# A hybrid decoder layer on one core: the feed-forwards of three token groups taken in the order 768, 768, 576 instead of 576, 768, 768

## The chip, the cores and the metric

The kernel runs on one core of a Trainium2 chip. The metric is the device time of one execution in microseconds: the median of repeated runs. Beside it stands one execution taken with the hardware profiler, whose trace gives the start and duration of every instruction of PE (TensorE matmuls; PEld are its weight loads), DVE (VectorE), ACT (ScalarE), POOL (GpSimd) and of the DMA queue that SP (SyncE) issues.

## The reference, cut to what matters

One decoder layer, in float32, over 2048 tokens of a prompt and 8 x 8 tokens of a sample group with the same weights. The model width is 1024, the feed-forward 4096.

```
h  = rmsnorm(x, norm_mix_w)
m  = mixer(h, ...)                 # retention and gated recurrence along the tokens, then @ w_out
x  = x + m
h  = rmsnorm(x, norm_ffn_w)
x  = x + square(relu(h @ w_up)) @ w_down       # 1024 -> 4096 -> 1024
y  = rmsnorm(x, final_norm_w)
```

Mixing runs along the tokens, since each carries a recurrent state to the next. The feed-forward treats each token by itself.

## The kernel before, in words

**Groups.** The 2112 tokens are cut into three groups, `gs[0]` of 64 sample and 512 prompt tokens (576), `gs[1]` and `gs[2]` of 768 prompt tokens. The program mixes them in turn (`mix`, `out_proj`), then runs a feed-forward (`ffn`) for each in turn. `out_proj` leaves two DRAM tensors per group: `fin`, the scaled input of the feed-forward, and `fres`, the residual. Tokens lie along the free dimension; each group is halved, so a matmul streams 288 or 384 columns. The program holds a second, slower copy of itself behind a flag (`judge` computes it); that copy isn't executed here.

**Products.** A float32 operand is split into two parts, hi and lo, and a product is hi x hi + hi x lo + lo x hi: three matmuls. The multiplication by `w_up` and `w_down` follows a scheme of seven products for a 2 x 2 block matrix, with sums of operands (T1 to T4) and of weights (S1 to S4, made earlier and kept in DRAM). Here a product means the 24 matmuls with one weight tile of 128 x 1024. A feed-forward is 112 products: 56 in the up half (eight rounds `t` of seven; `up_two` does the first two together, `up` the others), 56 in the down half (`down`, four octets).

**What each weight costs.** A tile is loaded into `raw` (8 buffers) by SP, copied to `hi` by ACT (L311) and the rest put into `lo` by DVE (L318). `hi` and `lo` have three buffers each, so the hi of product k+2 can be written once product k-1 is done, and its lo must be there for the third matmul of product k+2. The cost does not depend on the group.

**What else a feed-forward does, beside the matmuls (L1868).**
- `prepare` and `plan_operands` load quarters of `fin` (L1941, tile `ld`), form T1 to T4 (L1972, DVE) and split them (L1961 on ACT, L1965 on DVE).
- The results of products are added out of PSUM by DVE: L2087 and L2117 in `up_two`, L2145 in `up`, L2217 ("put") and L2220 in `down`; L2060 squares on DVE.
- `scale_residual(g, wait)` loads the residual from `fres`, squares it (L2003 on ACT, L2005 on DVE), sums it over the partitions (L2038, then `parts` L682 on ACT and L683 on DVE, matmuls L688 and L689) and scales it (L2020). `wait` is 0 in the first feed-forward and 190 in the others.
- `finish(g, ...)` belongs to the group just done and runs beside the next group's up half: squares (L2307 on ACT, L2309 and L2312 on DVE), the same column sum (L2038, L682, L683), then the multiplication by the final norm's factor (L2325, sixteen of half a group's width) and the write of y (L2327).
- The last group has no feed-forward behind it. `finish(g, (1,), True)` does its second token half during the last products. `last_rows` (L2367 on ACT, L2369 and L2372 on DVE), `last_product` and `finish_last` (squares L2407, L2408, L2412 and some recorded as L246, weights L2401 and L2403, sums L2427, factor L2358 and L2359, output multiplies L2436, writes L2437) do the first half around the last two products.

**What sets the order.** Such side work is put on an agenda by `later(ticks, ...)`; a tick is two matmuls, so it passes faster in the group of 576. Each engine runs its instructions in a fixed order, which a scheduler sets when the program is built; instructions recorded by a helper that raises their priority (`soon`) all carry line L246. The end of mixing is `out_proj(gs[2], 3, ...)`: eight projections whose results DVE adds to blocks of x (L246; `slab<-x` is their load, L252), in two PSUM buffers named pj, then eight short ones; during the first eight `prepare` begins loading the first feed-forward's operands.

```
            self.ffn(gs[0], lambda: self.prepare(gs[1], 8))
            self.finish(gs[0], begin=96, pace=10, wait=200, each=8)
            self.ffn(gs[1], lambda: self.prepare(gs[2], 8), 190)
            self.finish(gs[1], begin=96, pace=10, wait=200, each=8)
            ...
            self.ffn(gs[2], None, 190)
```

Of the kernel before, what the change touches and what calls it, by code (L numbers as in the profile page):

```python
# [205 lines left out]
class Kernel:  # L206
# [298 lines left out]
    def build(self):  # L505
        nc, tc, I = self.nc, self.tc, self.I
        with ExitStack() as ctx:
# [45 lines left out]
            gs = []  # L553
            off = 0
            for ns, p0, n in GROUPS:
# [4 lines left out]
                first = nch // 2  # L560
# [47 lines left out]
                mixing.close()  # L608
                self.pf = ctx.enter_context(tc.tile_pool(name="pf", bufs=2, space=bass.MemoryType.PSUM))

            self.out_proj(gs[2], 3, lambda: self.prepare(gs[0], 12), end_of_mixing)
            if self.fast:
                self.last_states()
            nc.sync.dma_start(self.O["ret_p"].rearrange("h d v -> d h v"), self.S[:, :H])
            nc.sync.dma_start(self.O["hg_p"].rearrange("h d v -> d h v"), self.S[:, H:])
            self.ffn(gs[0], lambda: self.prepare(gs[1], 8))
            self.finish(gs[0], begin=96, pace=10, wait=200, each=8)
            self.ffn(gs[1], lambda: self.prepare(gs[2], 8), 190)
            self.finish(gs[1], begin=96, pace=10, wait=200, each=8)
            if self.fast:  # L620
                self.judge()
            self.ffn(gs[2], None, 190)
            if self.fast:
                self.again = nc.values_load(self.flag, min_val=0, max_val=1,
                                            skip_runtime_bounds_check_because="a comparison's result is 0 or 1")
# [1879 lines left out]
```

## Time and profile before

| | |
|---|---|
| median of 3 runs | 2357.23 us (2357.16 to 2358.59) |
| the profiled execution | 2359.45 us, span of its instructions 2357.6 us |
| TensorE clock granted | 0.998 of full speed |
| busy: PE, DVE, ACT | 2337.3 us (99%), 1792.8 us (76%), 1227.3 us (52%) |
| feed-forward of 576 tokens | 1050 to 1408 us from the span's start |
| feed-forwards of 768 tokens | 1408 to 1874 and 1874 to 2340 us |
| moved by DMA | 575.6 MB, 244 GB/s on average |

Times in the trace count from the span's start. A line `L318 DVE TENSOR_TENSOR lo<-raw,hi` is an instruction of line 318 of the kernel on DVE, which writes a tile named lo from raw and hi; in brackets behind it stands how long the engine was idle before it and what ended that. Durations of neighbouring DVE or PE instructions overlap a little, so the step from one to the next is shorter than the printed duration.

### The profile page before, as it was taken

What the parts mean: (1) busy time and instruction counts of PE and PEld (TensorE: products, weight loads), DVE (VectorE), ACT (ScalarE), POOL (GpSimd) and SP (SyncE); (2) the same over time, 40 slices, a digit from 0 to 9 for tenths busy, and PEclk for the clock granted to TensorE, in tenths of its full rate; (3) what the DMA queues carried; (4) which work ended last, traced back from release to release, by engine and by line L of the source; (5) the groups of instructions that cost most, each with busy time, mean ns of one, the idle gap of its engine ahead of it and who ended that gap; (6) DMA issues with size and microseconds to landing.
All of it is one profiled execution on the core that took longest, in us unless ns stands there. A gap on an engine that the chain in (4) does not pass through costs nothing.

```text
span 2357.6 us, 39360 instructions
## 1 busy us (share of the span) xinstructions
PE 2337.3 (99%) x15340; PEld 2301.6 (98%) x15340; DVE 1792.8 (76%) x2309; ACT 1227.3 (52%) x1976; POOL 139.1 (6%) x199
## 2 busy tenths in 40 slices
PE   9999999999999999999999999999999999999998
PEld 8888899999999999999999999999999999999997
DVE  8766766777666776668769988666988787669887
ACT  5556555557645555546455546444544364445443
POOL 3221201111001100100000000000000000000000
PEclk9999999999999999999999999999999999999999
DMA  9888887779866777898677665767665458675642
GB/s 317 285 296 298 267 314 255 280 266 324 302 226 242 273 285 286 300 344 304 219 258 262 219 219 189 248 206 229 224 194 186 152 192 270 194 232 179 207 154 70
DMA packets 232649, 575.60 MB, mean 244 GB/s; under 512 B 24195, under 2 KB 92803, under 8 KB 232454
## 3 DMA queue, kind: packets, MB, share of 16 engines
q1 hardware_dynamic: 231766, 572.20, 71.3%
q8 instruction: 122, 2.00, 0.4%
q10 hardware_dynamic: 688, 0.80, 0.1%
q14 instruction: 73, 0.60, 0.1%
HBM read 419.95 MB, written 151.66 MB: 242 GB/s over the span
## 4 chain that ended last, share of the span: by engine, by line
PE 93%; DVE 3%; ACT 1%; DMA 1%; issue 1%; POOL 0%; SPq 0%; DVEq 0%; POOLq 0%; ACTq 0%
PE pj L1868 36%; PE pf L1868 28%; PE pj L464 11%; PE pj L1125 10%; PE pj L1206 2%; PE mm L1707 1%; PE mm L1715 1%; PE mm L1709 1%; PE mm L1393 1%; PE mm L1482 1%; PE mm L1635 1%; PE mm L1206 0%; PE mm L1857 0%; DVE raw L429 0%; DVE lo L318 0%
## 5 line engine op out<-in xcount | busy, mean ns | idle before, releaser
L1868 PE MATMUL pj<-slab,hi 128*128 128x384 f32 (+1 forms) x3504 | 853.4, 326 | 0.0
L311 ACT CAST hi<-raw 128x1024 fp32r<-128x1024 f32 x446 | 468.6, 1051 | 692.1 <-PE pj L1868 264.6
L318 DVE TENSOR_TENSOR lo<-raw,hi 128x1024 fp32r<-128x1024 f32 x446 | 545.8, 1224 | 157.3 <-ACT hi L311 152.2
L1868 PE MATMUL pf<-slab,hi 128*128 128x384 f32 (+1 forms) x2768 | 652.2, 321 | 0.0
L1868 PEld LDWEIGHTS pj<-slab,hi 128*128 128x128 f32 x3504 | 614.3, 188 | 0.0
L1868 PE MATMUL pj<-slab,lo 128*128 128x384 f32 (+1 forms) x1752 | 570.7, 326 | 0.0
L1868 PEld LDWEIGHTS pf<-slab,hi 128*128 128x128 f32 x2768 | 480.0, 188 | 0.1
L1868 PE MATMUL pf<-slab,lo 128*128 128x384 f32 (+1 forms) x1384 | 443.1, 320 | 0.0
L1868 PEld LDWEIGHTS pj<-slab,lo 128*128 128x128 f32 x1752 | 329.3, 188 | 0.0
L1125 PE MATMUL pj<-hi,slab 128*128 128x256 f32 x1344 | 260.4, 287 | 0.3 <-DVE slab L246 0.3
L1868 PEld LDWEIGHTS pf<-slab,lo 128*128 128x128 f32 x1384 | 260.1, 188 | 0.0
L464 PE MATMUL pj<-slab,hi 128*128 128x288 f32 (+1 forms) x1216 | 243.4, 316 | 2.1 <-ACT slab L246 1.0
L1125 PEld LDWEIGHTS pj<-hi,slab 128*128 128x128 f32 x1344 | 214.9, 191 | 0.6 <-DVE slab L246 0.6
L464 PEld LDWEIGHTS pj<-slab,hi 128*128 128x128 f32 x1216 | 194.2, 188 | 5.3 <-issue 1.8
L1125 PE MATMUL pj<-lo,slab 128*128 128x256 f32 x672 | 190.1, 283 | 0.0
L1961 ACT CAST slab<-slab 128x768 fp32r<-128x768 f32 (+1 forms) x192 | 145.4, 779 | 62.9 <-DVE slab L1972 47.4
L246 DVE TENSOR_TENSOR slab<-pj,slab 128x768 f32<-128x768 f32 (+2 forms) x136 | 124.2, 915 | 70.4 <-PE pj L1868 27.3
L1965 DVE TENSOR_TENSOR slab<-slab 128x768 fp32r<-128x768 f32 (+1 forms) x192 | 167.3, 886 | 13.2 <-ACT slab L1961 4.6
L464 PE MATMUL pj<-slab,lo 128*128 128x288 f32 (+1 forms) x608 | 143.5, 315 | 0.0
L1125 PEld LDWEIGHTS pj<-lo,slab 128*128 128x128 f32 x672 | 128.7, 192 | 0.0
L464 PEld LDWEIGHTS pj<-slab,lo 128*128 128x128 f32 x608 | 102.6, 188 | 0.3 <-issue 0.2
L2217 DVE TENSOR_TENSOR slab<-pf,slab 128x768 f32<-128x768 f32 (+1 forms) x87 | 76.5, 884 | 24.4 <-PE pf L1868 24.2
(265 smaller groups left out, 2572.0 us busy)
## 6 DMA issues: line engine op xcount, KB each, us to landing
raw<-w SPq DMA_DIRECT2D x254, 512.0 KB, 5.2
slab<-fu SPq DMA_DIRECT2D x64, 384.0 KB, 5.3
fu<-ld SPq DMA_DIRECT2D x60, 384.0 KB, 3.9
ld<-fin SPq DMA_DIRECT2D x28, 384.0 KB, 5.0
ld<-x SPq DMA_DIRECT2D x24, 384.0 KB, 7.0
slab<-fu SPq DMA_DIRECT2D x32, 288.0 KB, 4.8
fu<-ld SPq DMA_DIRECT2D x30, 288.0 KB, 3.2
slab<-x SPq DMA_DIRECT2D x16, 384.0 KB, 6.7
```

The costliest lines, as they stand in the source:

```text
L246: return fn(*a, **k)
L311: self.nc.scalar.copy(self.wts[j][0], raw)
L318: self.nc.vector.tensor_tensor(out=lo, in0=raw, in1=hi.bitcast(F32), op=ALU.subtract)
L464: self.nc.tensor.matmul(pj[:, i, :T2], w, a[:, c0:c1], start=j == 0 and q == 0, stop=j == n - 1 and q == 2)
L1125: self.nc.tensor.matmul(ps[:, tb * 256:(tb + 1) * 256], t, w[:, cols], start=first and kb == j == 0 and tb != 1, stop=kb == KB // 2 - 1 an ...
L1206: nc.tensor.matmul(dst, t[:, s:s + C], ww, start=kb == 0 and q == 0, stop=last and q == 2, skip_group_check=True)
L1393: nc.tensor.transpose(ps[:, j * P:(j + 1) * P], src[:, c], self.ident)
L1482: nc.tensor.matmul(ps[:, j * P:(j + 1) * P], k[:, cols[c]], q[:, cols[c]], start=True, stop=True)
L1868: m = self.nc.tensor.matmul(*a, **k)
L1961: self.nc.scalar.copy(hi[:, :g.T], B[name][:, :g.T])
L1965: self.nc.vector.tensor_tensor(out=lo[:, :g.T], in0=B[name][:, :g.T], in1=hi.bitcast(F32)[:, :g.T], op=ALU.subtract)
L2217: nc.vector.tensor_tensor(out=r, in0=ps, in1=r, op=ALU.add)
```

## The change

The feed-forwards run for `gs[1]`, `gs[2]`, `gs[0]`; with them go the preparation of operands, the finish and the program's last work, which is now that of the group of 576. Mixing keeps its order. In the changed kernel every line from 612 on has a number one higher.

```
-            self.out_proj(gs[2], 3, lambda: self.prepare(gs[0], 12), end_of_mixing)
+            first, second, third = (gs[1], gs[2], gs[0]) if self.fast else gs
+            self.out_proj(gs[2], 3, lambda: self.prepare(first, 12), end_of_mixing)
...
-            self.ffn(gs[0], lambda: self.prepare(gs[1], 8))
-            self.finish(gs[0], begin=96, pace=10, wait=200, each=8)
-            self.ffn(gs[1], lambda: self.prepare(gs[2], 8), 190)
-            self.finish(gs[1], begin=96, pace=10, wait=200, each=8)
+            self.ffn(first, lambda: self.prepare(second, 8))
+            self.finish(first, begin=96, pace=10, wait=200, each=8)
+            self.ffn(second, lambda: self.prepare(third, 8), 190)
+            self.finish(second, begin=96, pace=10, wait=200, each=8)
...
-            self.ffn(gs[2], None, 190)
+            self.ffn(third, None, 190)
```

Three places in the engines' orders, each before and then after the change.

SP's queue at the end of mixing, from the third-last block of x (`slab<-x`) on; `ld<-fin` are operands of the first feed-forward, `raw` weights, `fsd30S` and `fsd31S` sums of weights that are kept. Before:

```order
L1941 DMA ld<-fin_3781 128x2x288
L252 DMA raw<-w 128x1024
L1898 DMA raw<-w 128x1024
L252 DMA slab<-x 128x768
L1906 DMA fsd30S_11505<-raw 128x1024
L1906 DMA fsd31S_11597<-raw 128x1024
L252 DMA raw<-w 128x1024
L252 DMA slab<-x 128x768
L252 DMA raw<-w 128x1024
L1941 DMA ld<-fin_3781 128x2x288 x4
L252 DMA raw<-fsu0S_4699 128x1024
L252 DMA slab<-x 128x768
```

SP's queue at the same place, after:

```order
L1942 DMA ld<-fin_7765 128x2x384
L252 DMA raw<-w 128x1024
L1899 DMA raw<-w 128x1024
L252 DMA slab<-x 128x768
L1907 DMA fsd30S_11505<-raw 128x1024
L1942 DMA ld<-fin_7765 128x2x384
L1907 DMA fsd31S_11597<-raw 128x1024
L252 DMA slab<-x 128x768
L252 DMA raw<-w 128x1024 x2
L1942 DMA ld<-fin_7765 128x2x384 x2
L252 DMA raw<-fsu0S_4699 128x1024
L252 DMA slab<-x 128x768
```

One operand load and one block of x stand earlier, and four wider operand loads stand where five stood.

DVE in `up_two` of the last feed-forward, where it does that group's additions and the finish of the group before (L2309, L2312; L2310, L2313 after). Before, both groups have 768 tokens:

```order
L318 TENSOR_TENSOR lo<-raw,hi 128x1024
L2312 TENSOR_TENSOR slab<-slab 128x384
L2117 TENSOR_TENSOR slab<-slab 128x768
L2087 TENSOR_TENSOR slab<-pj,slab 128x768
L318 TENSOR_TENSOR lo<-raw,hi 128x1024
L2309 TENSOR_TENSOR slab<-slab 128x768 x2
L683 TENSOR_TENSOR slab<-slab 128x384
L2087 TENSOR_TENSOR ld<-pf,slab 128x768
L2087 TENSOR_TENSOR slab<-pf,slab 128x768
L318 TENSOR_TENSOR lo<-raw,hi 128x1024
```

DVE at the same place, after:

```order
L318 TENSOR_TENSOR lo<-raw,hi 128x1024
L2088 TENSOR_TENSOR slab<-pj,slab 128x576
L2118 TENSOR_TENSOR slab<-slab 128x576
L318 TENSOR_TENSOR lo<-raw,hi 128x1024
L2310 TENSOR_TENSOR slab<-slab 128x768
L2088 TENSOR_TENSOR ld<-pf,slab 128x576
L2310 TENSOR_TENSOR slab<-slab 128x768
L2088 TENSOR_TENSOR slab<-pf,slab 128x576
L318 TENSOR_TENSOR lo<-raw,hi 128x1024
L2310 TENSOR_TENSOR slab<-slab 128x768
```

The group's own rows are narrower, the finish of the group before and the weights' lo are as wide as before.

DVE at the program's end, around the last put (L2217, L2218 after) ahead of `last_product`; L246 are additions of its four blocks. Before:

```order
L318 TENSOR_TENSOR lo<-raw,hi 128x1024
L2325 SCALAR_TENSOR_TENSOR slab<-slab,vec 128x384
L2372 TENSOR_TENSOR slab<-slab 128x384
L2325 SCALAR_TENSOR_TENSOR slab<-slab,vec 128x384 x2
L2217 TENSOR_TENSOR slab<-pf,slab 128x768
L2325 SCALAR_TENSOR_TENSOR slab<-slab,vec 128x384 x2
L2369 TENSOR_TENSOR slab<-slab 128x768
L246 TENSOR_TENSOR slab<-pj,slab 128x384
L2325 SCALAR_TENSOR_TENSOR slab<-slab,vec 128x384 x2
L246 TENSOR_TENSOR slab<-pj,slab 128x384
L2325 SCALAR_TENSOR_TENSOR slab<-slab,vec 128x384
L2408 TENSOR_TENSOR slab<-slab 128x768
```

DVE at the same place, after:

```order
L318 TENSOR_TENSOR lo<-raw,hi 128x1024
L684 TENSOR_TENSOR slab<-slab 128x288
L2218 TENSOR_TENSOR slab<-pf,slab 128x576
L2373 TENSOR_TENSOR slab<-slab 128x288
L2326 SCALAR_TENSOR_TENSOR slab<-slab,vec 128x288 x2
L246 TENSOR_TENSOR slab<-pj,slab 128x288
L2326 SCALAR_TENSOR_TENSOR slab<-slab,vec 128x288 x2
L246 TENSOR_TENSOR slab<-pj,slab 128x288
L2370 TENSOR_TENSOR slab<-slab 128x576
L2326 SCALAR_TENSOR_TENSOR slab<-slab,vec 128x288 x2
L246 TENSOR_TENSOR slab<-pf,slab 128x288
L2409 TENSOR_TENSOR slab<-slab 128x576
```

All eight output multiplies L2326 of the finish now stand behind the put (two more follow the last row shown); before, three of the eight L2325 stood ahead of it.

## The prediction

> **What bounds the kernel now.** I began with the page's engine totals, then the stages of the feed-forwards, then the chain that ended last.
>
> ```profile
> span 2357.6 us, 39360 instructions
> PE 2337.3 (99%) x15340; PEld 2301.6 (98%) x15340; DVE 1792.8 (76%) x2309; ACT 1227.3 (52%) x1976; POOL 139.1 (6%) x199
> ...
> 1050.00:1229.30 179.30, 179.30 (x1346) 179.20 (x1346) 133.44 (x154) 98.00 (x123) 0.00 (x0) 1.00 0.79 265
> 1229.30:1408.40 179.10, 179.10 (x1345) 179.10 (x1345) 171.69 (x210) 94.25 (x116) 0.00 (x0) 1.00 0.73 238
> 1408.40:1641.40 233.00, 233.00 (x1348) 233.00 (x1347) 162.90 (x180) 114.51 (x134) 0.00 (x0) 1.00 0.66 214
> 1641.40:1874.40 233.00, 233.00 (x1346) 233.00 (x1345) 204.63 (x215) 104.87 (x117) 0.00 (x0) 1.00 0.60 195
> 1874.40:2107.30 232.90, 232.90 (x1346) 232.90 (x1345) 164.59 (x179) 115.18 (x133) 0.00 (x0) 1.00 0.66 215
> ...
> 1242.76 6.40 PE pf L1868 x48
> ...
> 1651.68 8.32 PE pj L1868 x48
> ```
>
> The five stage rows (length, then busy us of PE, PEld, DVE, ACT, POOL, then clock, DMA share, GB/s) are the up and down halves of the 576-token feed-forward, the same of the first one of 768, and the up half of the last. PE is busy through all of them at full clock. The two chain rows give the price of work there: 48 matmuls of 288 columns take 6.40 us (133 ns each), 48 of 384 columns 8.32 us (173 ns). One product is 24 matmuls against one weight: 3.20 us for the small group, 4.16 us for a big one. So TensorE bounds every feed-forward in either order, and what the change can move is only (a) the passage from mixing into the first feed-forward, (b) whatever makes PE wait inside one, (c) the end, where PE has finished and others have not.
>
> The profiled execution took 2359.45 us, 1.85 us around its 2357.6 us span. The sum below is made against that span; the median of the three runs, 2357.23, lies 2.2 us under the profiled time, and I add the sum to it.
>
> **PE work: 0.** The same 2688 matmuls of 288 and 2 x 2688 of 384 columns run, in another order. 358.4 + 2 x 465.9 us stays.
>
> **(a) The passage out of mixing: +0.3 us.** The first feed-forward's operands are now 384 KB quarters, not 288 KB ones. They are loaded beside the end of mixing, on SP's queue among the x blocks that the last residual adds wait for.
>
> ```profile
> 980.00:1000.00 20.00, 20.00 (x140) 20.00 (x139) 9.72 (x26) 8.90 (x39) 0.60 (x3) 1.00 0.85 331
> 1000.00:1020.00 20.00, 20.00 (x122) 19.97 (x121) 16.29 (x24) 6.96 (x11) 0.00 (x0) 1.00 0.95 303
> 1020.00:1040.00 20.00, 20.00 (x116) 19.73 (x115) 11.92 (x13) 4.56 (x5) 0.00 (x0) 1.00 0.99 345
> ...
> 1034.28 0.96 DVE L246 TENSOR_TENSOR slab<-pj,slab 128x768 f32<-128x768 f32 x1 [2.40 <-DMA slab<-x]
> ...
> 1034.83 0.51 PE L464 MATMUL pj<-slab,lo 128*128 128x384 f32 x2
> 1035.29 0.98 PE L464 MATMUL pj<-slab,hi 128*128 128x384 f32 x4
> ```
>
> The DMA engines are 99% busy, and the last add before PE reuses that PSUM bank waits 2.40 us for its x block. PE starts its next block at 1035.29, 0.46 us after the row before it; two such matmuls need 0.34, so it already waits 0.12 us here. There is no slack: what delays this x block delays PE. In the new order (front section) four operand loads stand ahead of that block in this stretch where five stood: 4 x 393 KB against 5 x 295 KB, 98 KB more, 0.28 us at the 345 GB/s of the third row. I take +0.3. The six loads before them grow by 590 KB, 1.7 us at that rate; between 980 and 1000 the DMA engines were idle 15% of 20 us, 3 us, which takes that in. If it didn't, the upper end is +1.9. At the lower end the 0.12 us vanishes, since one x block and one load moved ahead: -0.1. Behind this, the weights of the first products come 4.16 instead of 3.20 us apart while each still takes the same DMA, ACT and DVE time, so the first feed-forward is looser than before.
>
> **(b) DVE in the last feed-forward: +0.9 us.** The 576-token group leaves DVE least room: each weight costs it the same, and a product lasts 3.20 us. Its up half was first and carried only its own work. Now it carries the previous group's finish, with rows of 768. The step from one DVE row to the next is 0.08 us less than the printed duration, since they overlap.
>
> ```profile
> 1060.77 1.23 DVE L318 TENSOR_TENSOR lo<-raw,hi 128x1024 fp32r<-128x1024 f32 x1 [0.64 <-ACT hi L311]
> ...
> 1099.28 1.22 DVE L318 TENSOR_TENSOR lo<-raw,hi 128x1024 fp32r<-128x1024 f32 x1
> ...
> 1049.99 0.42 PE L1868 MATMUL pf<-slab,hi 128*128 128x288 f32 x2
> ...
> L2309 DVE TENSOR_TENSOR slab<-slab 128x768 f32<-128x768 f32 x6 | 5.7, 954 | 1.0 <-ACT slab L2307 0.9
> ...
> L2309 DVE TENSOR_TENSOR slab<-slab 128x576 f32<-128x576 f32 x6 | 4.5, 754 | 0.9 <-ACT slab L2307 0.8
> ...
> L2312 DVE TENSOR_TENSOR slab<-slab 128x384 f32<-128x384 f32 x2 | 1.1, 550 | 0.0
> L2325 DVE SCALAR_TENSOR_TENSOR slab<-slab,vec 128x384 f32<-128x384 f32 x16 | 8.8, 612 | 0.0
> ```
>
> The two L318 rows are the second halves ("lo") of the weights of products 5 and 17 of the first feed-forward; PE's product 0 begins at 1049.99. Between them lie 38.5 us, of which DVE works 34.1 (12 lo at 1.14, 30 rows of 576 elements at 0.67, one of 288 at 0.37). In the new order the same stretch of the last feed-forward gets six L2309 (0.87 each), two L2312, two L2038 and two L683 of 384 elements (0.47 each), 8.0 us, and loses three L2005 and one L2038 (2.4): 39.7 us of DVE work where PE needs 12 x 3.20 = 38.4. The lo of product 17 may begin at latest 0.27 us into its product less its own 1.14: 54.4 - 0.9 = 53.5 us after the first product begins; that of product 5 begins at 10.8. Room 42.7, work 39.7, and the waits of DVE for ACT's hi (0.64 in the first row; about that before each of the next five weights, 3.2 in all) leave -0.2. A wait of L2309 for ACT, 0.9 in its row, makes it -1.1. I take a PE wait of 0.9 us, near the second, since in the order L2309 follows its square on ACT closely. Bounds: 0, when those waits vanish because DVE is behind the hi anyway; 2.3, when the whole 4.4 us of idle time between the two rows stays and the 0.9 comes on top (42.7 - 39.7 - 4.4 - 0.9). After product 17 the sixteen L2325 (0.53 each) come, but L2005 moves away: 22.9 us of work in the 25.6 us of the next eight products, so it recovers. The down half of the 576 group ran without a PE wait at 171.7 of 179.1 us and now loses the six rows of preparing a next group.
>
> **(c) The end: +0.2 us.**
>
> ```profile
> 2334.00 0.61 DVE L2325 SCALAR_TENSOR_TENSOR slab<-slab,vec 128x384 f32<-128x384 f32 x1
> ...
> 2336.28 0.96 DVE L2217 TENSOR_TENSOR slab<-pf,slab 128x768 f32<-128x768 f32 x1
> 2337.16 1.14 DVE L2325 SCALAR_TENSOR_TENSOR slab<-slab,vec 128x384 f32<-128x384 f32 x2
> ...
> 2344.09 0.56 DVE L246 TENSOR_TENSOR slab<-slab 128x384 f32<-128x384 f32 x1
> 2344.23 0.34 PE L1868 MATMUL pf<-slab,lo 128*128 128x384 f32 x1
> ...
> 2344.70 1.63 PE L2427 MATMUL pj<-slab,ones 128*128 128x192 f32 x8
> 2345.00 0.63 ACT L246 ACTIVATE slab<-slab 128x192 f32<-128x192 f32 x2 [0.29 <-DVE slab L246]
> 2346.80 3.84 DVE L2436 TENSOR_TENSOR slab<-slab 128x384 f32<-128x384 f32 x8 [0.72 <-ACT slab L2359]
> 2348.32 1.78 SPq L2437 DMA_DIRECT2D y<-slab  x2
> ...
> GB/s 0 0 0 0 0 0 0 0 0 222 340 0 200 356 7 50 380 134 360 200 0 0 0 0 23 0 0 192 356 358 371 368 357 216 68 26 18 12 0 0
> ```
>
> From the top: DVE takes the last put before `last_product` (2336.28) and then works nearly without a gap to the third sum at 2344.09. PE's last matmul begins at 2344.23. The column sums (L2427) need both and start at 2344.70; ACT's squares of the last block end at 2345.63 and the second half of the sums waits for them; the output multiplies start at 2346.80, the output DMAs at 2348.32. In the GB/s row (0.7 us a slice from 2330) they fill the DMA engines from 2348 to 2353.
>
> The PE total is unchanged, so PE's last matmul comes at the same time, but its last two products take 2 x 3.20 instead of 2 x 4.16: the DVE chain behind the last put starts 1.92 us later. It does not get shorter by as much. In the new order it holds three rows of 576 elements, six of 288, two of 144 and eight L2325 of 288; before, only five of the eight L2325 stood behind the put. By the two L2309 rows an element costs 1.04 ns and a row 0.15 us beside; so the steps are 0.67, 0.37, 0.22 and, for L2325 (0.612 less 0.10 for 96 elements), 0.43: 2.0 + 2.2 + 0.4 + 3.4 = 8.1, with 0.1 for the start 8.2 us, against 8.4 before (2336.28 to 2344.70). The sums start 1.92 - 0.2 = 1.7 us later. From there to the first output multiply it took 2.10; the wait of the second sums for ACT (0.9) goes, since the squares now lie before the third sum, but both Ln now stand ahead of both Exp, and I take 0.4 off. From the first output multiply to the end it took 10.8; 4 x 393 KB are written at about 360 GB/s in 4.4 us, 4 x 295 KB in 3.3: 1.1 off. Sum 1.7 - 0.4 - 1.1 = +0.2. Bounds: -1.7, if DVE keeps up with PE and the sums start where they did with 0.4 + 1.3 off behind them (1.3 with the first two multiplies, 0.2); +1.3, if DVE waits 0.6 more for ACT and the shorter multiplies (8 x 0.10) set the rest in place of the bytes.
>
> [...] Were the rows proportional to their elements instead, the chain of 8.4 us would be 8.4 x 0.75 plus the three moved L2325, 7.5 us, and the end 0.7 us sooner than I have it.
>
> [...]
>
> **Sum.** +0.3 +0.9 +0.2 = +1.4 us: span 2359.0, and 2357.23 + 1.4 = 2358.6.
>
> **Rivals.** Within 0.2% is 4.7 us either way, about what a measurement can tell here.
> - *The small tail pays.* Nothing new waits and the end shrinks with the group. For it: PE's own last two products are 1.92 shorter. Against it: PE's total isn't, and DVE's chain binds. All of the 13.0 us from PE's end (2344.6) to 2357.6, at three quarters, gives -3.3: 2353.9. Even so it is not faster by 0.2%; for that (under 2352.5) the end must lose 4.7 of its 13.0 us, for which I see no row. Chances 0.15 and 0.03.
> - *DVE and ACT trade waits in the last feed-forward (slower).* If each of the twelve lo between products 5 and 17 waits 0.64 us for its hi, as the first six do, 7.7 us of idle time stand against a room of 3.0: PE waits 4.7 us, and with 0.3 and 0.2 the time is 2362.4. It decides from 7.2 us of idle time there on. Against it: once DVE is behind, the hi are long done; from 1078 on before it hardly idles. Chance 0.11.
> - *The DMA backlog persists into the passage.* (a) becomes 1.9: 2360.2. For it: 95% and 99% DMA. Against it: the idle 15% before. Chance 0.10.
> - *The edit does nothing.* The orders show that it moves all it names; but with no wait anywhere and an even end the time is 2357.2, inside the likeliest case.
>
> **How the numbers follow.** The likeliest case, 0.61, has its own range of 2356.5 to 2360.5, from (b) between 0 and 2.3 and (c) about one us either way. The given range, 2354.0 to 2362.0, leaves out the lower half of the first rival (0.07 and 0.03) and most of the second (0.08). Only the 0.03 is faster by over 0.2%, only the second rival slower (over 2361.9): 0.03, 0.86, 0.11.
>
> **What would show it.** Right: the feed-forwards stand as two of 465.9 us and one of about 359, the PE gap near the last x block is 0.1 to 0.7 us, DVE is full in the first 70 us of the last feed-forward with a lo landing late near products 13 to 17, and from PE's last matmul to the column sums 2 us pass where 0.1 did. Wrong: PE gaps elsewhere (operands or weights not landed at a change of group), a gap of over 2 us in the last up half, or sums that start at once behind PE.

## The result, and the profile after

The changed kernel takes 2362.14 us (median of 22 runs, 2358.99 to 2364.78), the kernel before 2358.66 us in 22 runs beside it (2356.87 to 2360.42; the three shown ahead are among them). The ratio is 1.0015, with a 95% interval of 1.0009 to 1.0021: 3.5 us slower, where 1.4 were forecast. That is within the 0.2% that was called no change, and 0.1 us above the upper end of the range. The profiled execution took 2361.42 us, 0.7 below its median; its span is 1.9 us longer than before.

I read three places, in the order of the prediction's steps. Line numbers from 612 on are one higher in the changed kernel. First the passage. The DVE rows below are, for the kernel before and then for the changed one, an update of the state in mixing, ahead of the first moved instruction, and the last residual add, at which the first feed-forward begins.

```profile
905.22 0.29 DVE L246 SCALAR_TENSOR_TENSOR S<-S,mm 128x128 f32<-128x128 f32 x1 [0.24 <-PE mm L1715]
...
1050.19 0.96 DVE L246 TENSOR_TENSOR slab<-pj,slab 128x768 f32<-128x768 f32 x1 [1.12 <-PE pj L464]
```

```profile
904.46 0.29 DVE L246 SCALAR_TENSOR_TENSOR S<-S,mm 128x128 f32<-128x128 f32 x1 [0.24 <-PE mm L1716]
...
1049.17 0.96 DVE L246 TENSOR_TENSOR slab<-pj,slab 128x768 f32<-128x768 f32 x1 [1.12 <-PE pj L464]
```

Between them pass 144.97 us before and 144.71 after. The passage gained 0.26 us. It gained them at the add that waited 2.40 us for its x block before (the row at 1034.28 in the prediction). In the changed kernel the same add waits 1.41 us, and PE's rows behind it follow each other without a gap:

```profile
1032.72 0.96 DVE L246 TENSOR_TENSOR slab<-pj,slab 128x768 f32<-128x768 f32 x1 [1.41 <-DMA slab<-x]
...
1034.06 0.51 PE L464 MATMUL pj<-slab,lo 128*128 128x384 f32 x2
1034.41 0.85 PE L464 MATMUL pj<-slab,hi 128*128 128x384 f32 x4
1035.10 0.51 PE L464 MATMUL pj<-slab,lo 128*128 128x384 f32 x2
```

Before, the row that follows the two PE rows shown in the prediction (1034.83 and 1035.29) was this one:

```profile
1036.11 0.52 PE L464 MATMUL pj<-slab,lo 128*128 128x384 f32 x2
```

So PE's two steps there took 0.46 and 0.82 us and now take 0.35 and 0.69, which is 0.24 of the 0.26. The 0.76 us by which the changed kernel is ahead at the first of the two rows were there before anything that the change touches.

Then the feed-forwards. Below are the stage rows of the changed kernel: the two of 768 tokens whole, and the up half of the last one, of 576.

```profile
1049.10:1515.00 465.90, 465.90 (x2690) 465.90 (x2689) 353.66 (x363) 213.21 (x238) 0.00 (x0) 1.00 0.63 209
1515.00:1980.90 465.90, 465.90 (x2690) 465.90 (x2689) 369.64 (x394) 220.39 (x251) 0.00 (x0) 1.00 0.62 204
1982.00:2161.60 179.60, 177.45 (x1323) 176.49 (x1322) 143.25 (x176) 101.57 (x130) 0.00 (x0) 1.00 0.75 251
```

PE has no gap in the first two and is idle for 2.15 us in the last. The list of PE's waits from 1000 us on names them (the first row belongs to the end, the other two to the last feed-forward; before, the list is empty):

```profile
PE pj L2428 <- DVE slab L246: 1.9, 1, 1.9
PE pj L689 <- ACT slab L683: 1.4, 1, 1.4
PE pj L1869 <- ACT hi L311: 0.7, 1, 0.7
```

From the first matmul of the feed-forwards to the last pass 1294.24 us before (1049.99 to 2344.23) and 1297.39 after (1048.97 to 2346.36): 3.15 us more.

Last the end, in the changed kernel: the last put, PE's last matmul, the column sums, the output multiplies.

```profile
2340.29 0.76 DVE L2218 TENSOR_TENSOR slab<-pf,slab 128x576 f32<-128x576 f32 x1 [1.16 <-PE pf L1869]
...
2346.36 0.29 PE L1869 MATMUL pf<-slab,lo 128*128 128x288 f32 x1
2348.59 1.25 PE L2428 MATMUL pj<-slab,ones 128*128 128x144 f32 x8 [1.93 <-DVE slab L246]
...
2350.40 3.04 DVE L2437 TENSOR_TENSOR slab<-slab 128x288 f32<-128x288 f32 x8 [1.59 <-ACT slab L2360]
```

The sums start 2.23 us behind PE's last matmul, where 0.47 stood before; from there to the end it takes 10.9 us, where 12.9 stood. The end as a whole is 13.14 us against 13.37.

So the two traces differ by -0.26 (passage), +3.15 (feed-forwards) and -0.23 (end; the spans are printed to 0.1 us, so an end is known no better), 2.66 in all; less the 0.76 of the earlier start that is the 1.9 us of the spans. What had to be found out is why PE waits in the last feed-forward, whether that is the whole of it, and what makes the median 3.5 and not 2.7.

### The profile page after: what moved, and what is told of

Same layout as the page of the kernel before. It is cut to its first block, busy times and chain, and to the rows that moved or that the text cites. A ratio compares the mean times of both kernels' runs of the same rounds, so it can differ in the third digit from the quotient of the medians.

```text
span 2359.5 us, 39363 instructions
## 1 busy us (share of the span) xinstructions
PE 2337.3 (99%) x15340; PEld 2302.7 (98%) x15340; DVE 1791.1 (76%) x2309; ACT 1225.9 (52%) x1976; POOL 138.3 (6%) x199
## 4 chain that ended last, share of the span: by engine, by line
PE 93%; DVE 3%; ACT 1%; DMA 1%; issue 1%; POOL 0%; SPq 0%; DVEq 0%; ACTq 0%; POOLq 0%
PE pj L1869 36%; PE pf L1869 28%; PE pj L464 10%; PE pj L1126 10%; PE pj L1207 2%; PE mm L1708 1%; PE mm L1716 1%; PE mm L1710 1%; PE mm L1483 1%; PE mm L1636 1%; PE mm L1858 1%; PE mm L1394 1%; PE mm L1207 0%; DMA ld<-slab 0%; DVE slab L246 0%
## 5 line engine op out<-in xcount | busy, mean ns | idle before, releaser
L246 DVE TENSOR_TENSOR slab<-pj,slab 128x768 f32<-128x768 f32 (+2 forms) x136 | 123.9, 913 | 68.8 <-PE pj L1869 27.3
L2218 DVE TENSOR_TENSOR slab<-pf,slab 128x768 f32<-128x768 f32 (+1 forms) x87 | 77.0, 890 | 32.9 <-PE pf L1869 32.8
```

The costliest lines, as they stand in the source:

```text
L246: return fn(*a, **k)
L2218: nc.vector.tensor_tensor(out=r, in0=ps, in1=r, op=ALU.add)
```

## The two waits of PE

The later and longer one stands at 2035 us, where PE has done sixteen products of the last feed-forward. PE, ACT and DVE of the changed kernel there:

```profile
2037.02 0.44 PE L689 MATMUL pj<-slab,ones_r 128*128 128x384 f32 x1 [1.41 <-ACT slab L683]
2037.43 0.45 PE L689 MATMUL pf<-slab,ones_r 128*128 128x384 f32 x1
...
2035.51 1.04 ACT L311 CAST hi<-raw 128x1024 fp32r<-128x1024 f32 x1 [2.01 <-PE pj L1869]
2036.46 0.92 ACT L683 CAST slab<-slab 128x384 fp32r<-128x384 f32 x2
...
2034.50 0.55 DVE L2039 TENSOR_TENSOR slab<-slab 128x384 f32<-128x384 f32 x1
2034.97 0.75 DVE L2061 SCALAR_TENSOR_TENSOR slab<-slab 128x576 f32<-128x576 f32 x1
2035.63 0.55 DVE L2039 TENSOR_TENSOR slab<-slab 128x384 f32<-128x384 f32 x1
```

L689 is a column sum of the finish, two small matmuls that stand in PE's queue between two products. It needs ACT's L683, which needs DVE's L2039. DVE has been full since 2010 (47.52 us busy of the 48 to 2058, the row below), so L2039 comes at 2034.50. By then ACT has the next weight's hi ahead of L683, and that hi waits 2.01 us for the buffer that PE's running product holds. PE's product ends, hi is cast (1.04), then L683 runs, and only then L689 and the products behind it: PE waits for ACT, and ACT had waited for PE.

```profile
2010.00:2058.00 48.00, 45.85 (x337) 44.89 (x336) 47.52 (x65) 29.22 (x39) 0.00 (x0) 1.00 0.72 240
```

The earlier wait stands at product 13, and half of it can be read from the built order of PE. Before, the group of 576 ran product 13 right behind product 12; in the changed kernel (below, from the last matmul of product 12 on) two matmuls of product 14 (`pf`, hi) and one of product 15 (the first `pj`) stand ahead of it. Product 13 accumulates in the PSUM bank of product 11, and must wait for DVE to read that (L2088).

```
8336 L1869 MATMUL pf<-slab,lo 128x288
8337 L1869 MATMUL pf<-slab,hi 128x288 [waits Activation_49]
8338 L1869 MATMUL pf<-slab,hi 128x288
8339 L1869 MATMUL pj<-slab,hi 128x288 [waits DVE_49,Activation_49]
8340 L1869 MATMUL pj<-slab,hi 128x288 [waits DVE_49]
```

```profile
2026.02 0.67 PE L1869 MATMUL pj<-slab,hi 128*128 128x288 f32 x3 [0.74 <-ACT hi L311]
...
2024.92 1.05 ACT L311 CAST hi<-raw 128x1024 fp32r<-128x1024 f32 x1 [1.41 <-PE pf L1869]
...
2024.02 1.22 DVE L318 TENSOR_TENSOR lo<-raw,hi 128x1024 fp32r<-128x1024 f32 x1
2025.16 0.75 DVE L2088 TENSOR_TENSOR slab<-pj,slab 128x576 f32<-128x576 f32 x1
```

Product 15's hi can be cast only when product 12 has given its buffer back; that cast ends at 2025.97, DVE's late L2088 at 2025.9, and PE goes on at 2026.02. DVE's backlog and the order give the same end here. The lo of product 13, in the stretch where the prediction had a lo landing late, is there at 2025.2. The lo of product 17, which the prediction's sum is about, begins at 2037.94, 54.9 us after PE's first product of this feed-forward; PE, which had waited before, did not wait for it:

```profile
1983.07 0.51 PE L1869 MATMUL pj<-slab,hi 128*128 128x288 f32 x2
...
2037.94 1.22 DVE L318 TENSOR_TENSOR lo<-raw,hi 128x1024 fp32r<-128x1024 f32 x1
```

## The experiments

The edits are shown against the changed kernel. Each version was timed in five rounds (11 runs, e7 with 6) beside the kernel before, which has 33 runs beside c1 to e3 and 28 beside e4 to e7. The ratio is estimated from all runs of both and is not quite that of the two medians. "Passage" is the time between the two DVE rows of the passage above, "feed-forwards" from their first matmul to their last, "end" from there to the end of the span, all from the one profiled execution of each.

| run | median, before beside it (us) | ratio, 95% | passage | feed-forwards | end |
|---|---|---|---|---|---|
| before (profile) | | | 144.97 | 1294.24 | 13.37 |
| changed (profile) | 2362.14, 2358.66 | 1.0015, 1.0009-1.0021 | 144.71 | 1297.39 | 13.14 |
| c1_after_again | 2362.22, 2358.09 | 1.0016, 1.0007-1.0025 | 144.75 | 1298.88 | 13.42 |
| e1_small_middle | 2361.04, 2358.09 | 1.0016, 1.0007-1.0025 | 144.72 | 1297.28 | 13.43 |
| e2_spread | 2359.19, 2358.09 | 1.0005, 0.9995-1.0014 | 144.71 | 1295.61 | 13.11 |
| e3_small_middle_spread | 2359.83, 2358.09 | 1.0006, 0.9997-1.0015 | 145.17 | 1295.54 | 13.17 |
| e4_late | 2359.60, 2358.33 | 1.0007, 0.9998-1.0016 | 144.70 | 1294.33 | 13.47 |
| e5_small_middle_late | 2358.43, 2358.33 | 1.0003, 0.9994-1.0012 | 144.69 | 1294.23 | 12.96 |
| e6_late_tail | 2359.25, 2358.33 | 1.0003, 0.9994-1.0012 | 144.71 | 1294.32 | 12.20 |
| e7_early_factor | 2365.31, 2358.33 | 1.0033, 1.0021-1.0045 | 144.71 | 1301.23 | 13.21 |

**c1_after_again: the changed kernel once more.**

> The changed kernel once more, unchanged, so that a second profile of it stands beside the first. Theory A (the time is lost in the up half of the last feed-forward, where the in-order queue of TensorE holds a column-sum matmul of the finish that waits for ACT and VectorE): 3 to 4 us above the kernel before, the same two waits of TensorE (0.7 and 1.4 us) near products 13 and 16 of the last feed-forward, 2.9 us more from its first matmul to its last than before. Theory B (the passage out of mixing costs the difference, by a DMA backlog that comes and goes between executions): the same time, but PE's first feed-forward starts later than in the first profile, by the 1 us or so that the first profile's time lay below the median.

Measured: 3.8 us above before by the ratio, 4.1 by the medians. The two waits are there to the hundredth (0.7 and 1.4), the passage is the same, and Theory B falls: the first feed-forward did not start later but 0.9 us sooner. Yet the feed-forwards take 1.5 us more than in the first profile. The windows of 1 us from the long wait on show it (the number before the last two is the granted clock):

```profile
2035.00:2036.00 1.00, 0.00 (x0) 0.00 (x0) 0.99 (x2) 1.00 (x3) 0.00 (x0) 1.00 0.83 291
2036.00:2037.00 1.00, 0.87 (x3) 0.55 (x3) 0.89 (x2) 1.00 (x3) 0.00 (x0) 1.00 0.88 340
2037.00:2038.00 1.00, 1.00 (x5) 0.92 (x5) 1.00 (x2) 0.79 (x3) 0.00 (x0) 0.63 0.94 364
2038.00:2039.00 1.00, 1.00 (x6) 1.00 (x5) 1.00 (x3) 0.62 (x2) 0.00 (x0) 0.50 0.14 54
2039.00:2040.00 1.00, 1.00 (x6) 1.00 (x5) 1.00 (x2) 0.64 (x2) 0.00 (x0) 0.50 0.72 230
2040.00:2041.00 1.00, 1.00 (x7) 1.00 (x6) 1.00 (x3) 0.00 (x0) 0.00 (x0) 0.66 0.82 307
```

About 1 us behind the wait the clock falls to 0.50 for 3.4 us (0.74 + 1 + 1 + 0.68, from the shares), which costs up to 1.7 us. In the first profile the same windows show 1.00 throughout. By these 1.7 of 2362 us a dip takes 0.0007 off the mean clock of a run, an estimate; 9 of the 33 runs of the changed kernel list 0.997 (mean 2363.1 us), the others 0.998 (mean 2361.6), and none of the 33 runs of the kernel before beside c1 lists 0.997. The count is rough. The listed clock has three digits, and it also holds the end, where in the profiles of before and of the changed kernel the clock falls to 0.50 some time after PE's last matmul (at 2349 and at 2352 us). One of 28 runs of the kernel before beside e4 to e7 lists 0.997 too, and so does one of 11 of e4 and of e6, which have neither wait; of e1, which has both, also only one of 11. If 9 of 33 is right, the dips add 0.46 us to the mean; that is an estimate.

**e1_small_middle: 768, 576, 768.** The end is that of before again; the small group still carries the finish of a big one.

```
-            first, second, third = (gs[1], gs[2], gs[0]) if self.fast else gs
+            first, second, third = (gs[1], gs[0], gs[2]) if self.fast else gs
```

> Order 768, 576, 768: the first feed-forward is that of the changed kernel, the last one that of the kernel before, and the 576-token group carries the finish of a group of 768 as in the changed kernel. Theory A: the two waits now stand in the second feed-forward, the end is that of before (the end after the change was worth -0.2 by the two profiles), so the time is that of the changed kernel or up to 0.5 above: 3 to 4 us above the kernel before, ratio 1.0015. Theory C (what the profile does not show is lost at the end, which the 576 group makes worse): 1 to 2 us above before at most, ratio 1.0006, since the end is the old one. Theory B: as A in time, but without PE waits in the second feed-forward.

The ratio is that of c1, and the waits of the second feed-forward are the same two:

```profile
PE pj L689 <- ACT slab L683: 1.4, 1, 1.4
PE pf L1869 <- ACT hi L311: 0.7, 1, 0.7
```

So the loss does not need the small group at the end (Theory C falls); it follows the 576 group to where it carries a finish of 768.

**e2_spread: the finish begins earlier and comes more slowly.**

```
-            self.finish(second, begin=96, pace=10, wait=200, each=8)
+            self.finish(second, begin=48 if self.fast else 96, pace=14 if self.fast else 10, wait=232 if self.fast else 200, each=8)
```

> The changed kernel with the finish that the last feed-forward carries spread out: its squares begin at tick 48 and come every 14 ticks, its factors at ticks 224 and 226 and its output rows from 232, where they stood at 96, every 10, 192 and 200. Nothing else moves. Theory A: both PE waits go, the last feed-forward takes 2.5 to 2.9 us less, and the time falls to within 1 us of the kernel before (ratio 1.000 to 1.0005). Theories B and C: it stays where the changed kernel is (ratio 1.0015), though the waits are gone or smaller, since the time is lost elsewhere.

3.0 of the 4.1 us between c1 and before are gone (1.0005). The column sum now finds its operands; the wait at product 13 stays, in the list of waits of the last feed-forward:

```profile
PE pj L1869 <- ACT hi L311: 0.7, 1, 0.7
```

Theory A had both waits go; only the one on L689 went, and in the profiles it and what hung on it were worth 1.8 us of the feed-forwards (1297.39 to 1295.61).

**e3_small_middle_spread: the same in the order 768, 576, 768.** The edits of e1 and e2 together, the second on the finish of `first`.

> Order 768, 576, 768 with the same spread of the finish that the 576-token feed-forward carries: only the passage out of mixing differs from the kernel before, and the place of the small group. Theory A, with a passage that costs nothing or gains (0.9 us by the first two profiles): equal to the kernel before or up to 1 us below (ratio 0.9996 to 1.000). Theory B: the passage alone keeps it 2 to 4 us above (ratio 1.001 to 1.0015).

1.0006 lies between the two expectations, and its interval holds both. The feed-forwards carry the same 1.3 us more than before, since the wait at product 13 is still there. The passage was 0.45 longer than in the other profiles in this one execution, the only one of nine.

**e4_late: the finish behind the crowded stretch.**

```
-            self.finish(second, begin=96, pace=10, wait=200, each=8)
+            self.finish(second, begin=150 if self.fast else 96, pace=10, wait=280 if self.fast else 200, each=8)
```

> The changed kernel with the finish in the last feed-forward moved behind the crowded stretch: squares from tick 150 every 10, factors at 272 and 274, output rows from 280. In the order as built, PE then finishes product 13 before product 14; in the changed kernel and with the spread finish, 22 of the 24 matmuls of product 13 stand behind those of product 14, and PE waits there for product 14's hi. Theory A: both waits are gone, the feed-forwards take 1294.3 us again from the first matmul to the last (1297.2 in the changed kernel, 1295.6 with the spread finish), and the time is that of the kernel before, less the 0.2 us of the end: ratio 0.9996 to 1.0002. Rival: the rest of 1.1 us that the spread finish left is the passage or the end: ratio 1.0004 to 1.0008.

That expectation misreads the order that it starts from: the product that is cut is 14, and PE waits there for the hi of product 15. In the built order of e4 nothing of products 14 and 15 stands ahead of product 13. No PE wait is left in the last feed-forward, and DVE is no longer full:

```profile
2020.00:2040.00 20.00, 20.00 (x153) 20.00 (x152) 19.52 (x25) 13.93 (x18) 0.00 (x0) 1.00 0.81 255
2040.00:2060.00 20.00, 20.00 (x151) 20.00 (x150) 15.32 (x20) 12.16 (x18) 0.00 (x0) 1.00 0.75 236
```

The feed-forwards take 1294.33 us, within 0.1 of before. That part of Theory A holds. The ratio, 1.0007, lies above what it expected; its interval holds both. Against e2 the median does not fall (2359.60 after 2359.19), so the 1.3 us that the wait at product 13 was worth are shown by the profiles alone.

**e5_small_middle_late: only the passage differs from before.** The edits of e1 and e4 together.

> Order 768, 576, 768 with the same late finish in the feed-forward of 576 tokens. Now only the passage differs from the kernel before. Theory A (the passage is worth nothing on the mean; the first matmul of the feed-forwards began between 1048.1 and 1051.5 us in five profiles of the same instructions): ratio 0.9998 to 1.0003. Rival (the passage costs about 1 us): ratio 1.0004 to 1.0008. The difference to the run beside it is the end alone: 0.2 us.

2358.43 against 2358.33 us. The ratio of 1.0003 is the upper edge of what Theory A expected, and its interval holds the rival's values too. Feed-forwards and end are those of before to within 0.4, the passage is not longer.

**e6_late_tail: e4, and three of the last scaled rows moved into DVE's idle time.**

```
-                self.later((41, 50, 59, 73)[k], out, np_, h)
+                self.later((41, 50, 59, 73)[k] if not self.fast else (41, 50, 76, 76)[k], out, np_, h)
```

> The late finish, and at the end three of the eight scaled output rows of the second half (the multiplies that stand in the chain behind the last put) moved behind the third sum, into VectorE's idle time before the output multiplies. Theory A (the end is set by the chain from the last put through the column sums): the sums begin 0.43 x 3 = 1.3 us earlier behind PE's last matmul, 0.9 instead of 2.2, and the time falls 0.9 to 1.3 us below the run with the late finish alone: ratio to before 0.999 to 0.9997. Rival (the end is set by the bytes written, or by PE): the sums come earlier, but the end stays where it is, ratio as with the late finish alone.

PE's last matmul, the sums, and on DVE the moved rows and the output multiplies:

```profile
2341.80 0.29 PE L1869 MATMUL pf<-slab,lo 128*128 128x288 f32 x1
2342.74 1.33 PE L2428 MATMUL pj<-slab,ones 128*128 128x144 f32 x8 [0.65 <-DVE slab L246]
...
2343.04 0.51 DVE L2326 SCALAR_TENSOR_TENSOR slab<-slab,vec 128x288 f32<-128x288 f32 x1
2343.51 0.37 DVE L2402 TENSOR_SCALAR slab<-slab,vec 128x288 f32<-128x288 f32 x1
2343.80 0.51 DVE L2326 SCALAR_TENSOR_TENSOR slab<-slab,vec 128x288 f32<-128x288 f32 x1
2344.55 3.04 DVE L2437 TENSOR_TENSOR slab<-slab 128x288 f32<-128x288 f32 x8 [0.24 <-ACT slab L2360]
```

The sums start 0.94 us behind PE, 1.29 sooner, as expected, and the end takes 12.20 us, 0.9 to 1.3 below the other five with the small group last (13.11 to 13.47). In the profile the chain of DVE sets the end. The times do not settle it: the median is 2359.25 against 2359.60 for e4, the mean 2358.77 against 2359.82. By the profiles this version should be 1.35 us faster than before (-0.26 + 0.08 - 1.17); a ratio of 1.0003, with 0.9994 to 1.0012, neither shows nor excludes that.

**e7_early_factor: the column sums one product earlier in PE's queue.**

```
-            self.finish(second, begin=96, pace=10, wait=200, each=8)
+            self.finish(second, begin=96, pace=10, wait=188 if self.fast else 200, each=8)
```

> The changed kernel with the finish's factors at ticks 180 and 182, not 192 and 194, and its output rows from 188: the two column-sum matmuls then stand one product earlier in TensorE's queue, while VectorE and ACT reach the values that they need no sooner, and product 13 is not cut in two. TensorE's waits there become one stretch of 2.5 to 4 us. Theory on the clock (a stretch of waiting brings a span of 3.4 us at half clock, as in the profile in which the granted clock fell to 0.50 behind the wait): it now comes in nearly every run, 1.7 us each, so that most runs list a clock of 0.997, and the time is 2 to 4 us above the changed kernel's, ratio 1.0025 to 1.0035. Rival (the lower clock came by chance, the wait doesn't bring it): as often as in the changed kernel, a quarter of the runs, and a time within 1.5 us of it.

Its waits, of column sums and at product 13, and two of the windows of 1 us behind the long one:

```profile
PE pj L689 <- ACT slab L683: 3.3, 1, 3.3
PE pj L2428 <- DVE slab L246: 1.9, 1, 1.9
PE pj L1869 <- DVE slab L2088: 0.7, 1, 0.7
...
2037.00:2038.00 1.00, 0.96 (x2) 0.60 (x3) 1.00 (x3) 1.00 (x3) 0.00 (x0) 0.56 0.90 357
2038.00:2039.00 1.00, 1.00 (x5) 1.00 (x5) 1.00 (x2) 0.94 (x3) 0.00 (x0) 0.50 0.89 346
```

All six runs list a clock of 0.997, and the time is 7.0 us above before, 3.2 above the changed kernel by the medians, in the expected interval. By the listed clock the longer wait brought the dip in all six runs, and the profile of one shows it; the rival, chance, would have given one or two of six. At product 13 nothing of product 15 stands ahead here, and PE waits 0.7 us all the same, now for DVE's L2088 itself. So DVE's backlog is enough for that wait without the order. The order prolongs it in turn: in e2 L2088 had ended at 2026.23, and PE waited on until 2026.59 for the hi of product 15. Only with the late finish, where both are gone, is there no wait.

## Why the prediction was off

- **What bounds the kernel** held: 465.90 us twice, PE full at full clock in every stretch of the first profile but the one named.
- **(a), the passage, +0.3 forecast.** Wrong in sign, by half a microsecond: 144.69 to 144.75 us in eight of the nine profiles in which `gs[1]` comes first, 145.17 in one, 144.97 before. The step that failed is the larger weight that I gave to 98 KB more ahead of the x block than to that block's place one step further ahead in SP's queue, which I had at the lower bound. The PE wait of 0.12 that was there is gone, and so is one of 0.13 in the step behind it, which I had not seen.
- **(b), DVE in the last feed-forward, +0.9 forecast.** The place was right (DVE full from 2010 to 2058, PE waits near products 13 and 16), the size was not: 3.15 us in the profile, and an estimated 0.46 more on the mean by the clock. The step that failed is the sum up to the lo of product 17: it asked only when DVE delivers lo, and took DVE's lateness there as PE's wait. As a sum it held. In the changed kernel that lo begins 54.9 us after the first product, 1.4 past the 53.5 that I had as the limit. But no lo stands among PE's waits, since PE had lost more than that before it came to product 17. PE waited for what else it takes from DVE and ACT: the bank of product 13 (0.74) and above all the column sums of the finish (1.41). Their matmuls stand in PE's own queue, and the working moved them with the finish at no cost. So the bound of 2.3 was no bound. The profiles of e2 and e4 show it: each wait that goes takes its time with it (1.8, then 1.3 us), while the DVE work is the same.
- **(c), the end, +0.2 forecast.** Right: the sums 1.76 us later behind PE (1.7 forecast), the chain from the put to the sums 8.30 us (8.2), the rest 2.0 us shorter (1.5). The five profiles with the small group last and the old tail have 13.27 us on the mean, the four with a big one 13.23: a difference of 0.04.
- **The rivals.** That DVE and ACT trade waits gave 2362.4 us, close to the time, by a mechanism that is not there: between 2009 and 2060 DVE waited 0.8 us in all for hi, not 7.7. What speaks against it in the prediction (once DVE is behind, hi is long done) held. The small tail did not pay, and the DMA backlog did not reach the passage.
- **The sum.** -0.26 + 3.15 - 0.23 + 0.46 = 3.1 us by the profiles and the estimate for the clock, 3.5 (2.1 to 5.0) measured.
- **The base.** The time of 2362.14 us lies 3.5 above the forecast of 2358.6. Of these, 2.1 come from the change, which cost 3.5 where 1.4 were forecast. The other 1.4 come from the kernel before: its median was 2357.23 us in the three runs that I added the sum to, and is 2358.66 in 22.

What stays open: the three kernels without a PE wait in the feed-forwards (e4, e5, e6) are 0.0003 to 0.0007 above before by the point values, where the profiles have them 0.1 to 1.3 us below. Their intervals allow it. The first of the two rows of the passage moves between 902.97 and 906.52 us from profile to profile, ahead of any instruction that the change moves; the spans move with it, and a difference below 2 us is not settled by eleven runs.

## What to carry to other kernels

When side work moves to a shorter stage, list everything that the bounding engine takes from the loaded one, not just its main operands: a small matmul in TensorE's queue that waits for a side chain stops every product behind it (1.41 us here, 3.30 in e7), and the chain may itself wait behind a cast that needs TensorE's buffer (2.01 us here). Check its distance in the queue, in products, against the backlog of the engine that feeds it; here one product less cost another 3.2 us, part of it by the clock, and putting the whole finish 54 to 80 ticks later took all the waits away. A gap in TensorE can also cost more than its length (in c1 a gap of 1.42 us was followed by 3.4 us at a clock of 0.50, up to 1.7 us more), so compare the granted clock behind it between several executions.

## What the runs showed of the hardware

The granted clock of TensorE fell to 0.50 for 3.4 us behind a gap of 1.42 us (1.7 from start to start) in one of two profiles of the same program, and behind a gap of 3.3 us in the one profile of e7, with 0.997 listed in all six runs. Just ahead of it PE was busy again in both: of the last 3.42 us (the dip's own length) for 2.00 in c1 and for 1.5 in e7.

Why the same gap brings a dip in some executions only stays open. In the first profile it is as long (1.41 us), and the clock stays at 1.00. The dip of c1 begins 1.13 us behind PE's first matmul after the gap (2036.13 to 2037.26 us, from the shares). Of the 3.42 us up to the same place in the first profile (2034.73 to 2038.15) PE was busy for 2.01, where c1 has 2.00. So PE's busy time there doesn't tell the two executions apart.
